# A state-space model rewritten as one real scan, and run as a third stream beside attention and RWKV

## The chip, the cores and the metric

The kernel runs on one core of one Trainium2 chip. The time is that of one execution on the device, in microseconds; the figure used is the median of the runs. Five engines work side by side, each with its own queue in a fixed order: PE (TensorE, matrix products, with its weight loads shown as PEld), DVE (VectorE), ACT (ScalarE), POOL (GpSimd) and SP, which here only starts transfers. A tool that simulates the program's time line puts every instruction into its engine's order when the program is built; on the chip this order doesn't change any more.

## The reference

One layer of a streaming encoder for 1024 prompt tokens and 32 sample tokens (1056 together), in f32. One input projection feeds three mixers; their outputs (384, 256 and 384 columns) go through one output projection, a norm, an MLP with squared ReLU of width 4096, and a second norm.

The mixer that changes is the S5 state-space model: 16 groups of 16 channels, each group with 64 complex states.

```
lam_bar = exp(lam * dt)                       # complex, one per state
x_t = lam_bar * x_{t-1} + B_bar u_t           # per group; zero start for the prompt, state_s5 for the sample
y_t = Re(C x_t) + D u_t
z = gelu(y);  out = z * sigmoid(z @ w_glu + b_glu)
```

The other two are latent attention with 6 heads, chunk-causal over the prompt and over 512 cached keys for the sample, and RWKV-7, a recurrence over a 64 x 64 matrix per head for 6 heads. The last states of S5 and RWKV are outputs too.

## The kernel before

A front part multiplies the input by all weight columns (f32 split in a high and a low half, three products each, `mm3`) and prepares the operands of the three mixers; they are left in DRAM: `u_d` for S5, `rw_d` for RWKV, `q_d` for attention's queries. `stage_s5_params` (L408) works out S5's constants in the same time: the time axis is cut in pieces of `L5` = 8 tokens, so that a group has 128 rows (16 channels x 8 tokens) and `NC5` = 132 columns (128 pieces of the prompt, 4 of the sample). It leaves `em_d` (input piece to state), `cl_d` (state to output piece) and `kt_d` (the kernel inside a piece) in DRAM, and the powers of lam_bar^8 in `g.lp`.

`rwkv_inv` (L764) then inverts the triangular blocks that RWKV needs.

`stage_s5` (L580) follows: all 16 groups at once. It loads `u`, `em`, the blocks `tz0` and `cl`; 16 products (L608) give each piece's contribution to the state, and ACT copies it out of PSUM twice, the second time with the real and imaginary halves of the partitions exchanged (L609, L611). DVE and POOL then run the complex recurrence over 128 pieces as a tree: `fold` (L627) inside runs of 4 and of 16 pieces, eight `advance` steps (L645) across, and back down (L669 to L683). Two products per group (L698, L699) give the output; gelu (L701), a trip through `z_d` that turns the layout, the gate products (L715), sigmoid (L717) and the final product (L719). The pool of this stage lies on the side of memory on which RWKV's pools `rp` and `rl` are opened afterwards.

Then two streams are traced alternately by `side_by_side` (L1291): `a`, `stage_mix`, is attention (233 steps of one tile of scores each: the row maxima of the next head between the outputs of this one); `b`, `stage_streams`, is RWKV (about 124 steps, nine tiles of up to 128 tokens). First `LEAD` steps of `a`, then `RATIO` steps of `a` for one of `b`. The steps of `b` get a higher priority in the planner, and a PE instruction of `a` may be issued only after the last PE instruction that `b` had `SLACK` = 3 steps ago. `attn_past` (L1080) prepares the cached keys. PSUM pools of this part: `psc` (2 buffers: score tiles for the maxima, tag `sc`), `pst` (2: score tiles for the output), `pav` (1) and `pr` (3, RWKV).

Near its end RWKV's stream loads the output weights (`out_weights`) into memory that RWKV no longer uses; `out_early` and `out_mm` start the output projection, and the MLP follows.

What waits on what around the change: RWKV's first loads `ld` (L832) and `xt` (L1030 to L1032) need the memory in which `rwkv_inv` and `stage_s5` worked; attention's memory lies on the other side. SP's queue carries, in one order, S5's loads and stores, RWKV's loads and stores, attention's queries and the row maxima that are written into them (L1246).

## Time and profile before

| | |
|---|---|
| median of 3 runs | 1626.97 us (1623.27 to 1628.03) |
| the profiled execution's own time | 1630.84 us |
| its span, first to last instruction | 1629.1 us |
| PE busy | 1501.1 us, 92% |
| DVE busy | 928.2 us, 57% |
| ACT busy | 501.3 us, 31% |
| POOL busy | 435.8 us, 27% |
| mean granted clock of PE | 0.954 |

The page gives, for each engine, the busy tenths in 40 slices of 40.7 us. The views used below are windows (busy time of each engine in a stretch of the span, with the clock granted to PE and the transfers), groups of instructions (line of the kernel, engine, operation, tiles and shapes; number; busy time and mean; then the idle time before them and what ended it), waits (who waited for whom: us in total, times, longest) and the time line (start, duration, engine, line). A matmul's end is modelled, so a busy PE need not be PE at its peak. An ACT, SP or POOL row with "q" after the name is a transfer being issued.

### The profile page before, as it was taken

The numbers are of one execution on the slowest core, as the hardware profiler recorded it, in microseconds if no ns is written. First come the engines' busy times: TensorE is split into PE (matmuls) and PEld (weight loads), VectorE is DVE, ScalarE is ACT, GpSimd is POOL, SyncE is SP. The second block draws the span as 40 slices with busy tenths as digits, with TensorE's granted clock in tenths as the row PEclk, the third lists the DMA queues.
The fourth block names the chain that finished last, engine by engine and source line by source line (L and its number), as shares of the span: only waits on it lengthen the run. The fifth ranks groups of instructions, "written<-read, shape, count | busy, mean of one in ns | idle before, by whom it ended". The sixth has DMA issues, their size and how long they took to land. (4 is left out here: it accounts for less than half of the span.)

```text
span 1629.1 us, 26187 instructions
## 1 busy us (share of the span) xinstructions
PE 1501.1 (92%) x10855; PEld 1351.0 (83%) x10855; DVE 928.2 (57%) x1644; ACT 501.3 (31%) x953; POOL 435.8 (27%) x385
## 2 busy tenths in 40 slices
PE   7899798957759999899899999999999999999995
PEld 6778797735538777677779999999999999999995
DVE  8535787158824565545765755545544555445457
ACT  4335433251444434343323122221111222221122
POOL 3713751453111021211412112221211122212123
PEclk9989899977789999999999999999999999999998
DMA  5313543540045122213612111111111111111012
GB/s 181 131 56 113 178 119 79 142 126 1 17 115 114 42 76 57 55 38 110 206 46 91 40 39 52 52 42 50 43 48 40 39 53 52 52 40 52 14 40 81
DMA packets 105259, 119.07 MB, mean 73 GB/s; under 512 B 48064, under 2 KB 82548, under 8 KB 104488
## 3 DMA queue, kind: packets, MB, share of 16 engines
q1 hardware_dynamic: 75796, 98.00, 19.8%
q10 hardware_dynamic: 29280, 19.20, 4.0%
q8 instruction: 85, 1.39, 0.3%
q14 instruction: 34, 0.28, 0.1%
q0 software_dynamic: 64, 0.20, 0.0%
HBM read 86.84 MB, written 30.48 MB: 72 GB/s over the span
## 5 line engine op out<-in xcount | busy, mean ns | idle before, releaser
L62 PE MATMUL acc<-xh,uphi 128*128 128x384 f32 (+1 forms) x768 | 248.9, 324 | 0.0
L64 PE MATMUL acc<-xl,uphi 128*128 128x384 f32 (+1 forms) x768 | 247.9, 323 | 0.0
L66 PE MATMUL acc<-xh,uplo 128*128 128x384 f32 (+1 forms) x768 | 247.6, 322 | 0.0
L1510 DVE TENSOR_TENSOR rl<-rl 128x384 f32<-128x384 f32 (+1 forms) x96 | 142.1, 1480 | 176.3 <-ACT rl L1509 174.8
L1538 DVE TENSOR_TENSOR yacc<-yacc,acc 128x384 f32<-128x384 f32 (+2 forms) x344 | 158.7, 507 | 111.8 <-PE acc L66 111.6
L62 PE MATMUL acc<-hh,dnhi 128*128 128x384 f32 (+2 forms) x736 | 209.2, 320 | 0.0
L64 PE MATMUL acc<-hl,dnhi 128*128 128x384 f32 (+2 forms) x736 | 207.1, 319 | 0.0
L66 PE MATMUL acc<-hh,dnlo 128*128 128x384 f32 (+2 forms) x736 | 197.4, 319 | 0.0
L49 POOL TENSOR_TENSOR dnlo<-dnraw,dnhi 128x1024 fp32r<-128x1024 f32 x30 | 72.1, 2404 | 336.4 <-ACT dnhi L48 320.7
L49 POOL TENSOR_TENSOR uplo<-upraw,uphi 128x1024 fp32r<-128x1024 f32 x34 | 82.1, 2416 | 248.7 <-ACT uphi L48 248.7
L62 PE MATMUL acc<-xh,wmhi 128*128 128x384 f32 (+3 forms) x384 | 133.6, 348 | 14.8 <-ACT xh L48 7.9
L62 PEld LDWEIGHTS acc<-xh,uphi 128*128 128x128 f32 x768 | 144.1, 188 | 0.3 <-ACT xh L48 0.3
L64 PEld LDWEIGHTS acc<-xl,uphi 128*128 128x128 f32 x768 | 144.2, 188 | 0.0
L66 PEld LDWEIGHTS acc<-xh,uplo 128*128 128x128 f32 x768 | 144.2, 188 | 0.0
L64 PE MATMUL acc<-xl,wmhi 128*128 128x384 f32 (+3 forms) x384 | 133.4, 348 | 2.7 <-DVE xl L49 2.7
L66 PE MATMUL acc<-xh,wmlo 128*128 128x384 f32 (+3 forms) x384 | 132.3, 345 | 0.0
L64 PEld LDWEIGHTS acc<-hl,dnhi 128*128 128x128 f32 x736 | 131.5, 188 | 0.0
L62 PEld LDWEIGHTS acc<-hh,dnhi 128*128 128x128 f32 x736 | 131.4, 188 | 0.0
L66 PEld LDWEIGHTS acc<-hh,dnlo 128*128 128x128 f32 x736 | 128.9, 188 | 0.0
L48 ACT ACTIVATE dnhi<-dnraw 128x1024 fp32r<-128x1024 f32 x30 | 31.8, 1060 | 298.2 <-PE acc L64 249.2
L48 ACT ACTIVATE hh<-rl 128x384 fp32r<-128x384 f32 (+1 forms) x96 | 47.9, 499 | 148.5 <-DVE rl L1510 148.5
L62 PEld LDWEIGHTS acc<-xh,wmhi 128*128 128x128 f32 (+1 forms) x384 | 74.6, 194 | 20.0 <-ACT xh L48 8.2
(490 smaller groups left out, 2963.7 us busy)
## 6 DMA issues: line engine op xcount, KB each, us to landing
upraw<-in_w_up SPq DMA_DIRECT2D x32, 512.0 KB, 3.6
dnraw<-in_w_dn SPq DMA_DIRECT2D x30, 512.0 KB, 3.6
ld<-rw SPq DMA_DIRECT2D x24, 320.0 KB, 3.9
wmraw<-in_w_m SPq DMA_DIRECT2D x12, 512.0 KB, 3.2
wo<-in_w_out SPq DMA_DIRECT2D x8, 512.0 KB, 3.7
z<-in_xa SPq DMA_DIRECT2D x8, 512.0 KB
out_y<-o SPq DMA_DIRECT2D x8, 512.0 KB, 2.6
xr<-in_xt SPq DMA_DIRECT2D x8, 384.0 KB, 6.3
```

Of the source, the lines that this page charges most:

```text
L48: nc.scalar.activation(out=hi, in_=ps, func=AF.Copy)
L49: (lo_eng or nc.vector).tensor_tensor(out=lo, in0=ps, in1=hi.bitcast(F32), op=ALU.subtract)
L62: nc.tensor.matmul(out=outs[i], lhsT=lh, rhs=rhs[i][0], start=start, stop=False)
L64: nc.tensor.matmul(out=outs[i], lhsT=lh, rhs=rhs[i][1], start=False, stop=False)
L66: nc.tensor.matmul(out=outs[i], lhsT=ll, rhs=rhs[i][0], start=False, stop=stop)
L1510: nc.vector.tensor_tensor(out=r[:, :n], in0=r[:, :n], in1=r[:, :n], op=ALU.mult)
L1538: nc.vector.tensor_tensor(out=y, in0=y, in1=ps[i][:, :n], op=ALU.add)
```

## The change

S5 is written anew as a generator, `stage_s5(g)`, that `stage_mix` steps inside attention's stream: after more than `S5_FROM` = 10 attention steps, one step of it follows every `S5_STEP` = 3rd. It has nine steps in each of its four rounds and ten behind them. It works on `NG` = 4 groups at a time, in four rounds, with one buffer for each of its three large tiles (`ut`: inputs and the blocks inside a piece; `em`: first the input matrix, then the output matrix; `ces`: the table of turns, states and outputs). Its pool lies on attention's side, so RWKV's pools come right behind `rwkv_inv`. `LEAD` goes from 90 to 15, `RATIO` from 1.3 to 2.0.

The recurrence: with lam_bar^8 = rho * e^(i phi), a table holds e^(-i k phi) for every piece k (doubling from 1 to 128, with one Newton step `unit` that keeps the length at 1 before each doubling from the second on). The pieces' contributions are multiplied by it, a real recurrence with rho is run over all pieces and groups by one `tensor_tensor_scan`, and the result is turned back. The columns of a group are the zero start, 128 pieces of the prompt, the sample's start state and 4 pieces of the sample (`NX` = 134; `NY` = 133 of them have an output); a factor of zero in the scan starts the prompt and the sample anew.

S5's PSUM tiles come from attention's `psc`. The output matrix is stored in another order of rows, by which the blocks inside a piece need no re-ordering by ACT; `z_d` is read back in 16 transfers instead of two. Gelu and the two sigmoids each switch ACT's table and back, without making later instructions wait for it (`keep=False`). The old chain of powers at the end of `stage_s5_params` gives way to three squarings of the unit turn. Small tiles move: attention's past tiles into tags `rec` and `rt`, RWKV's `so` into `m`, and the raw halves of every second output weight into S5's tile `ut`.

```diff
@@ -70,12 +70,13 @@
     return g.tc.issue_after(g.le) if g.le is not None else nullcontext()
 
 
-def log_exp_table(g, users):
+def log_exp_table(g, users, keep=True):
 
     pre = g.nc.scalar.preload_act_table_set("natural_log_exp_and_others")
     for u in users:
         g.tc.add_manual_dep(pre.ins, u.ins.name, mybir.DependencyInfo(mybir.DependencyClass.NoSync, mybir.DependencyReason.DATA), reason="table")
-    g.le = pre.ins
+    if keep:
+        g.le = pre.ins
 
 
 def rsqrt_newton(g, m, y, t):
@@ -426,6 +427,7 @@
     dt, mag, ang = t16("dt"), t16("mag"), t16("ang")
     nc.scalar.activation(out=dt, in_=ldt, func=AF.Exp)
     V.tensor_tensor(out=mag, in0=lre, in1=dt, op=ALU.mult)
+    nc.scalar.activation(out=g.rho, in_=mag, func=AF.Exp, scale=float(L5))
     nc.scalar.activation(out=mag, in_=mag, func=AF.Exp)
     V.tensor_tensor(out=ang, in0=lim, in1=dt, op=ALU.mult)
 
@@ -507,8 +509,8 @@
     V.tensor_scalar(out=pis, in0=pi, scalar1=-1.0, scalar2=None, op0=ALU.mult)
     cl = big("cl")
     tb = big("tb")
-    V.tensor_tensor(out=v4t(cl), in0=bc(cst[:, :, None, :], s4), in1=bc(prs[:, :, :, None], s4), op=ALU.mult)
-    nc.gpsimd.tensor_tensor(out=v4t(tb), in0=bc(csw[:, :, None, :], s4), in1=bc(pis[:, :, :, None], s4), op=ALU.mult)
+    V.tensor_tensor(out=v4(cl), in0=bc(cst[:, :, None, :], s4), in1=bc(prs[:, :, :, None], s4), op=ALU.mult)
+    nc.gpsimd.tensor_tensor(out=v4(tb), in0=bc(csw[:, :, None, :], s4), in1=bc(pis[:, :, :, None], s4), op=ALU.mult)
     V.tensor_tensor(out=cl[:, :2048], in0=cl[:, :2048], in1=tb[:, :2048], op=ALU.add)
     nc.scalar.dma_start(out=g.cl_d, in_=cl[:, :2048])
     c0 = sp.tile([P, G5, 16], F32, tag="c0", name="c0", bufs=1)
-    clf = v4t(cl)
+    clf = v4(cl)
@@ -550,174 +552,142 @@
-    pq = big("pq")[:, :512].rearrange("p (a n g) -> p a n g", a=2, n=16)
...
-    for n in (1, 2, 4, 8):
...
-def stage_s5(g, sp):
...
-        return sp.tile([P, G5 * NC5], F32, tag="b5", name=name, bufs=4)
...
-        nc.sync.dma_start(out=tz0[s:P:L5, :, 16 * s:P], in_=g.kt_d[:, :, 0:(8 - s) * 16])
...
-    def fold(x, y, n, c, eng=V):
...
-        V.tensor_tensor(out=t1, in0=x, in1=bcl(lam(n), [P, 2, G5, c]), op=ALU.mult)
...
-            V.tensor_tensor(out=y[:, w], in0=y[:, w], in1=t1[:, w], op=ALU.add)
...
-        fold(e4[:, :, :, :, j - 1], e4[:, :, :, :, j], 1, 32, nc.gpsimd)
...
-        fold(em4[:, :, :, :, 4 * m - 1], em4[:, :, :, :, 4 * m + 3], 4, 8)
...
-        advance(V, "p", ss[:, k + 1], ss[:, k], 16, em4[:, :, :, k, 15])
...
-        advance(nc.gpsimd, "s", sx[:, k + 1], sx[:, k], 1, ee[:, :, :, P + k])
...
-    log_exp_table(g, [nc.scalar.activation(out=zc, in_=zc, func=AF.Gelu_apprx_tanh)])
...
-    log_exp_table(g, [nc.scalar.activation(out=ot, in_=ot, func=AF.Sigmoid) for ot in ots])
...
+    c, q = a2[:, 16:32], a2[:, 0:16]
+    w2 = t16("w2")
+    for n in range(3):
+        V.tensor_tensor(out=w, in0=c, in1=c, op=ALU.mult)
+        V.scalar_tensor_tensor(out=w2, in0=q, scalar=2.0, in1=c, op0=ALU.mult, op1=ALU.mult)
+        V.tensor_tensor(out=q, in0=q, in1=q, op=ALU.mult)
+        V.tensor_tensor(out=c, in0=w, in1=q, op=ALU.subtract)
+        V.tensor_copy(out=q, in_=w2)
+    V.tensor_scalar(out=g.u5[:, 1], in0=q, scalar1=sgn, scalar2=-1.0, op0=ALU.mult, op1=ALU.mult)
+    V.tensor_copy(out=g.u5[:, 0], in_=c)
+    unit(g, g.u5, sp.tile([P, 2, G5], F32, tag="nrm", name="nrm", bufs=1))
+def unit(g, x, t):
+    V = g.nc.vector
+    V.tensor_tensor(out=t, in0=x, in1=x, op=ALU.mult)
+    V.tensor_tensor(out=t[:, 0], in0=t[:, 0], in1=t[:, 1], op=ALU.add)
+    V.tensor_scalar(out=t[:, 0], in0=t[:, 0], scalar1=-0.5, scalar2=1.5, op0=ALU.mult, op1=ALU.add)
+    V.tensor_tensor(out=x, in0=x, in1=bc(t[:, 0:1], list(x.shape)), op=ALU.mult)
+NG = 4
+NX = NC5 + 2
+NY = NC5 + 1
+def stage_s5(g):
+    sp = g.s5
+    for q in range(G5 // NG):
+        gs = slice(NG * q, NG * q + NG)
+        ut = sp.tile([P, NY * L5], F32, tag="ut", name="ut", bufs=1)
+        u = ut[:, :NG * NY].rearrange("p (g k) -> p g k", k=NY)
+        tz = ut[:, NG * NY:NG * NY + NG * P].rearrange("p (g x) -> p g x", x=P)
+        nc.gpsimd.memset(u[:, :, P:P + 1], 0.0)
+        nc.gpsimd.memset(tz, 0.0)
+        src = g.u_d[q // 2][64 * (q % 2):64 * (q % 2) + 64].rearrange("(g c) (t k) -> (c t) g k", c=16, t=L5)
+        nc.sync.dma_start(out=u[:, :, 0:P], in_=src[:, :, 0:P])
+        nc.sync.dma_start(out=u[:, :, P + 1:NY], in_=src[:, :, P:NC5])
+        em = sp.tile([P, NG, P], F32, tag="em", name="em", bufs=1)
+        nc.sync.dma_start(out=em, in_=g.em_d[:, gs])
+        for s in range(8):
+            nc.sync.dma_start(out=tz[s:P:L5, :, 16 * s:P], in_=g.kt_d[:, gs, 0:(8 - s) * 16])
+        ces = sp.tile([P, 4, NG * NX], F32, tag="ces", name="ces", bufs=1)
+        tb = ces.rearrange("p w (g k) -> p w g k", k=NX)
+        e, es = tb[:, 2], tb[:, 3]
+        t1, t2 = (ces[:, 2 + i, :NG * 128].rearrange("p (w g k) -> p w g k", w=2, g=NG) for i in range(2))
+        nc.gpsimd.memset(tb[:, 0, :, 0:1], 1.0)
+        nc.gpsimd.memset(tb[:, 1, :, 0:1], 0.0)
+        V.tensor_copy(out=tb[:, 0:2, :, 1], in_=g.u5[:, :, gs])
+        for n in (1, 2, 4, 8, 16, 32, 64):
+            if n > 1:
+                unit(g, tb[:, 0:2, :, n], sp.tile([P, 2, NG], F32, tag="nrm", name="nrm", bufs=1))
+            x, y = tb[:, 0:2, :, 1:n + 1], tb[:, 0:2, :, n + 1:2 * n + 1]
+            V.tensor_tensor(out=t1[:, :, :, :n], in0=x, in1=bc(tb[:, 0:1, :, n:n + 1], [P, 2, NG, n]), op=ALU.mult)
+            for w in range(2):
+                V.tensor_tensor(out=t2[:, w, :, :n], in0=x[:, 1 - w], in1=bc(tb[:, 1, :, n:n + 1], [P, NG, n]), op=ALU.mult)
+                V.tensor_tensor(out=y[:, w], in0=t1[:, w, :, :n], in1=t2[:, w, :, :n], op=ALU.add if w else ALU.subtract)
+            if n % 3 == 1:
+                yield
+        V.tensor_copy(out=tb[:, 0:2, :, P + 1:NX], in_=tb[:, 0:2, :, 0:5])
+        for j in range(0, NG, 2):
+            ps = g.psc.tile([P, 512], F32, tag="sc", name="s5e")[:, :2 * NY].rearrange("p (j k) -> p j k", k=NY)
+            for i in range(2):
+                nc.tensor.matmul(out=ps[:, i], lhsT=em[:, j + i], rhs=u[:, j + i], start=True, stop=True)
+            nc.scalar.activation(out=e[:, j:j + 2, 1:NX], in_=ps, func=AF.Copy)
+            for i in range(2):
+                nc.scalar.activation(out=es[hsl(1 - i), j:j + 2, 1:NX], in_=ps[hsl(i)], func=AF.Copy)
+            yield
+        nc.gpsimd.memset(tb[:, 2:4, :, 0:1], 0.0)
+        nc.gpsimd.tensor_copy(out=e[:, :, P + 1], in_=g.x0[:, 0, gs])
+        cl = sp.tile([P, NG, P], F32, tag="em", name="cl", bufs=1)
+        nc.sync.dma_start(out=cl, in_=g.cl_d[:, P * NG * q:P * NG * (q + 1)].rearrange("p (g x) -> p g x", x=P))
+        V.tensor_tensor(out=ces[:, 2:4], in0=ces[:, 2:4], in1=ces[:, 0:2], op=ALU.mult)
+        V.tensor_tensor(out=ces[:, 2], in0=ces[:, 2], in1=ces[:, 3], op=ALU.add)
+        nc.scalar.activation(out=es, in_=bc(g.rho[:, gs, None], [P, NG, NX]), func=AF.Copy)
+        nc.gpsimd.memset(es[:, :, 0:P + 2:P + 1], 0.0)
+        V.tensor_tensor_scan(out=ces[:, 2], data0=ces[:, 3], data1=ces[:, 2], initial=0.0, op0=ALU.mult, op1=ALU.add)
+            nc.scalar.activation(out=ces[hsl(1 - i), 3], in_=ces[hsl(i), 2], func=AF.Copy)
+        yield
+        V.tensor_tensor(out=ces[:, 2:4], in0=ces[:, 2:4], in1=ces[:, 0:2], op=ALU.mult)
+        V.tensor_tensor(out=ces[:, 2], in0=ces[:, 2], in1=ces[:, 3], op=ALU.subtract)
+        for i, k in enumerate((P, NX - 1)):
+            nc.gpsimd.tensor_copy(out=g.fin[:, i, gs], in_=e[:, :, k])
+        yo = ces[:, 3, :NG * NY].rearrange("p (g k) -> p g k", k=NY)
+        for j in range(0, NG, 2):
+            ps = g.psc.tile([P, 512], F32, tag="sc", name="s5y")[:, :2 * NY].rearrange("p (j k) -> p j k", k=NY)
+            for i in range(j, j + 2):
+                nc.tensor.matmul(out=ps[:, i - j], lhsT=tz[:, i], rhs=u[:, i], start=True, stop=False)
+                nc.tensor.matmul(out=ps[:, i - j], lhsT=cl[:, i], rhs=e[:, i, 0:NY], start=False, stop=True)
+            nc.scalar.activation(out=yo[:, j:j + 2], in_=ps, func=AF.Copy)
+            yield
+        nc.sync.dma_start(out=g.z_d[gs].rearrange("g x k -> x g k"), in_=yo)
+    so = sp.tile([P, NG, P], F32, tag="em", name="so", bufs=1).rearrange("p a b -> p (a b)")[0:G5, 0:256].rearrange("p (i s r) -> p i s r", i=2, r=2)
+    ps = g.psc.tile([P, 4, P], F32, tag="sc", name="s5l")
+    for i in range(2):
+        nc.tensor.transpose(out=ps[0:16, i], in_=g.fin[:, i], identity=g.ident)
+    yield
+    zt = sp.tile([P, 4, NG * NX], F32, tag="ces", name="zt", bufs=1).rearrange("p a b -> p (a b)")[:, :2 * L5 * NY]
+    zv = zt.rearrange("p (h t k) -> p h t k", h=2, t=L5)
+        for i in range(8):
+            nc.sync.dma_start(out=zv[16 * i:16 * i + 16, h], in_=g.z_d[8 * h + i].rearrange("(t c) k -> c t k", c=16))
+    wg = sp.tile([P, NG, P], F32, tag="em", name="wg", bufs=1).rearrange("p a b -> p (a b)").rearrange("p (k m) -> p k m", k=2)
+    log_exp_table(g, [nc.scalar.activation(out=zt, in_=zt, func=AF.Gelu_apprx_tanh)], False)
+    yield
+    for m in range(2):
+        om = sp.tile([P, NY * L5], F32, tag="ut", name="ot", bufs=1)
+        ot = om.rearrange("p (k t) -> p t k", t=L5)
+            ps = g.psc.tile([P, 512], F32, tag="sc", name="s5g")[:, :n * NY]
+                nc.tensor.matmul(out=ps, lhsT=wg[:, k, m * P:m * P + P], rhs=zt[:, (k * L5 + t) * NY:(k * L5 + t + n) * NY], start=k == 0, stop=k == 1)
+            nc.scalar.activation(out=ot[:, t:t + n], in_=ps.rearrange("p (t k) -> p t k", k=NY), func=AF.Identity, bias=g.vec[:, V_BGLU + m:V_BGLU + m + 1])
+            yield
+        log_exp_table(g, [nc.scalar.activation(out=om, in_=om, func=AF.Sigmoid)], False)
+        V.tensor_tensor(out=ot, in0=ot, in1=zv[:, m], op=ALU.mult)
+        nc.sync.dma_start(out=g.mg_d[3 + m, :, 0:TP], in_=om[:, 0:TP])
+        nc.sync.dma_start(out=g.mg_d[3 + m, :, TP:T], in_=om[:, TP + L5:TP + L5 + TS])
+        yield
@@ -969,7 +939,7 @@
-            so = g.rl.tile([64, 3, P], F32, tag="so", name="so", bufs=1)
+            so = g.rl.tile([P, 3, P], F32, tag="m", name="so", bufs=1)[0:64]
@@ -1074,7 +1044,8 @@
-RATIO, SLACK, PRIO, LEAD = 1.3, 3, 120, 90
+RATIO, SLACK, PRIO, LEAD = 2.0, 3, 120, 15
+S5_FROM, S5_STEP = 10, 3
@@ -1083,13 +1054,13 @@
-    ct = g.ap0.tile([P, 4, P], F32, tag="ct", name="ct")
+    ct = g.ap.tile([P, 4, P], F32, tag="rec", name="ct", bufs=1)
-    kt = g.ap0.tile([P, 4, 32], F32, tag="kt", name="kt")
+    kt = g.ap.tile([P, 4, 32], F32, tag="rt", name="kt", bufs=1)
@@ -1381,7 +1352,7 @@
-        raw = get("wst", 0, 1, dt=F32) if WOUT.index(k) % 2 else get("xt", 0, 3, dt=F32)
+        raw = g.s5.tile([P, NY * L5], F32, tag="ut", name="wo", bufs=1)[:, None, :1024] if WOUT.index(k) % 2 else get("xt", 0, 3, dt=F32)
@@ -1487,7 +1458,14 @@
-        yield from stage_attn(g)
+        ssm, n = stage_s5(g), 0
+        for _ in stage_attn(g):
+            yield
+            n += 1
+            if n > S5_FROM and n % S5_STEP == 0:
+                next(ssm, None)
+        for _ in ssm:
+            yield
@@ -1602,7 +1580,9 @@
-    g.lp = pool.tile([P, 3, 7, G5], F32, tag="lp", name="lp")
+    g.u5 = pool.tile([P, 2, G5], F32, tag="u5", name="u5")
+    g.rho = pool.tile([P, G5], F32, tag="rho", name="rho")
+    g.fin = pool.tile([P, 2, G5], F32, tag="fin", name="fin")
@@ -1623,7 +1603,7 @@
-    g.z_d = dram.tile([16, P, NC5], F32, tag="z_d", name="z_d")
+    g.z_d = dram.tile([16, P, NY], F32, tag="z_d", name="z_d")
@@ -1687,15 +1667,14 @@
+    g.s5 = s0.enter_context(tc.tile_pool(name="s5", bufs=1, reuse_waits="tile"))
-    with tc.tile_pool(name="s5", bufs=1, side="right", reuse_waits="tile") as sp:
-        stage_s5(g, sp)
-    attn_past(g)
+    attn_past(g)
```

122 lines of the change are left out of this document (removed).

## The prediction

> **What bounds the kernel now.** I read the page's slices first, then windows cut at the borders of the stages, then PE's waits. The kernel is bound by TensorE almost everywhere except in the slices from 330 to 490 us.
>
> ```profile
> span 1629.1 us, 26187 instructions
> ...
> PE   7899798957759999899899999999999999999995
> ...
> DVE  8535787158824565545765755545544555445457
> ...
> PEclk9989899977789999999999999999999999999998
> ```
>
> The windows below give, per stage, its length, then the busy time of PE, weight loads (PEld), DVE, ACT and POOL with instruction counts, the granted clock, and DMA. The SSM stage runs from 330 to 482 us beside the first 90 attention steps; RWKV starts at 482; from 490 to 735 RWKV and attention alternate; afterwards RWKV runs out alone.
>
> ```profile
> 330.00:345.00 15.00, 8.19 (x35) 5.22 (x36) 8.43 (x10) 10.08 (x17) 9.99 (x8) 0.77 1.10 327
> 345.00:482.00 137.00, 95.92 (x395) 68.44 (x393) 90.02 (x206) 56.42 (x101) 29.46 (x48) 0.82 0.10 30
> 482.00:490.00 8.00, 2.04 (x14) 1.33 (x14) 0.00 (x0) 0.26 (x1) 4.99 (x5) 0.50 1.28 202
> 490.00:735.00 245.00, 234.03 (x2936) 180.18 (x2931) 138.67 (x328) 104.07 (x234) 43.64 (x78) 0.97 0.25 64
> ```
>
> Until 490 us PE is busy 106.2 of 160 us, at a clock of about 0.82; in the alternating stretch it is busy 234.0 of 245 us (0.955) at 0.97. There the longest wait of PE is small:
>
> ```profile
> PE pry L958 <- ACT yb L937: 7.6, 2, 5.3
> ```
>
> So the early stretch is bound by the SSM's chain over DVE and ACT, the later one by PE. What the change can win is PE's empty time before 490.
>
> **The change, part by part.**
>
> *RWKV from the start, attention's lead cut from 90 steps to 15.* The total PE work is unchanged: same attention and RWKV matmuls; the SSM keeps its 16 state, 32 output and 12 gate products in nearly the same widths (133 columns for 132). The early work is slowed by the clock: 106.2 x 0.82 / 0.97 = 90 us at the later clock. The same score matmul shows it, in the first row before 482, in the second after:
>
> ```profile
> L64 PE MATMUL sc<-kl,qh 128*128 128x512 f32 (+5 forms) x41 | 16.0, 390 | 0.0
> ...
> L64 PE MATMUL sc<-kl,qh 128*128 128x512 f32 (+5 forms) x43 | 14.6, 340 | 0.0
> ```
>
> 90 + 234 = 324 us of work in what are now 405 us (330 to 735). At today's fill of 0.955 that takes 339 us: **-66 us**. At a fill of 1 it is -81; that is the far end.
>
> *The new start.* RWKV's memory now follows the triangular inverse, whose last store is the first row below; today RWKV's first matmul comes 8.1 us after the SSM's last store was issued.
>
> ```profile
> 330.69 3.80 ACTq L813 DMA_DIRECT2D xt_d<-zc  x2
> ...
> 335.19 3.78 PE L1131 MATMUL sck<-ckv,wkv 128*128 128x512 f32 x4 [6.61 <-ACT cpast L1091]
> ...
> 479.83 0.32 SPq L720 DMA_DIRECT2D mg_d<-ot  x1
> ...
> 487.96 0.69 PE L851 MATMUL pra<-ld 64*64 64x128 f32 x4 [13.13 <-DMA ld<-rw]
> ```
>
> 334.5 + 8.1 gives a first RWKV matmul near 343; until then PE has only attention's keys, from 335. Of the 15 us to 345 some 14.3 should be filled and about 4 will be: **+10** (8 to 12).
>
> *The SSM's DVE work.* The old state passes are sixteen DVE groups, 55.0 us in all, 4.1 of them the final gate product, which stays; the largest and the smallest:
>
> ```profile
> L635 DVE TENSOR_TENSOR ee<-ee,t 128x512 f32<-128x512 f32 (+1 forms) x12 | 9.3, 805 | 0.0
> ...
> L672 DVE TENSOR_TENSOR t<-t 128x256 f32<-128x256 f32 x3 | 1.2, 412 | 0.0
> ```
>
> The new work, by size, from these rows:
>
> ```profile
> L565 DVE TENSOR_TENSOR pq<-pq 128x16 f32<-128x16 f32 x1 | 0.2, 168 | 0.0
> ...
> L562 DVE TENSOR_TENSOR pq<-pq 128x64 f32<-128x64 f32 x1 | 0.2, 218 | 0.0
> ...
> L562 DVE TENSOR_TENSOR pq<-pq 128x128 f32<-128x128 f32 x1 | 0.3, 284 | 0.0
> ...
> L491 DVE TENSOR_TENSOR bb<-bb,t 128x256 f32<-128x256 f32 x1 | 0.4, 432 | 0.0
> ...
> L1276 DVE TENSOR_TENSOR rt<-rt,rec 64x512 f32<-64x512 f32 (+1 forms) x13 | 8.0, 617 | 1.6 <-ACT rec L1274 0.9
> ...
> L512 DVE TENSOR_TENSOR cl<-cl,tb 128x2048 f32<-128x2048 f32 x1 | 2.3, 2293 | 0.0
> ...
> L372 DVE TENSOR_TENSOR_SCAN cs<-m,cs x15: 222/675/702, 86.0 to 118.7; 128x260 f32<-128x260 bf16 x12, 128x33 f32<-128x33 bf16 x3
> ```
>
> The table of turns per round of four groups: 24 unit-length ops at 0.17 = 4.0 us; seven doublings with one op of 8 to 512 elements (2.1) and four of half that (6.5); two copies 0.3: 12.9 us. Then two products of 1072 elements (1.2 each), two sums of 536 (0.65), and a scan of 536: 0.22 us for 33 elements and 0.675 for 260 are 2.0 ns an element, so 1.23 us. Together 17.8 a round, 71 for four, 75 with the gate products: 20 us more than now.
>
> When it falls matters more. The SSM takes one step after every third attention step from the twelfth on, 46 steps, so it lives until about step 150 of 233: (150 - 15) / 218 = 0.62 of the shared stretch, some 210 us. DVE has 237.1 - 55.0 = 182 us of other work, 0.62 of it 113; with 75 it is 188 in 210 us, 0.9 of the time. The nearest rows are the five ten-microsecond windows of the present stretch in which DVE is busy over 8.2 us:
>
> ```profile
> 560.00:570.00 10.00, 9.92 (x178) 7.79 (x174) 9.34 (x19) 7.70 (x15) 0.55 (x4) 1.00 0.13 41
> 570.00:580.00 10.00, 8.01 (x80) 5.95 (x82) 8.71 (x22) 3.60 (x11) 4.37 (x5) 1.00 0.54 139
> ...
> 620.00:630.00 10.00, 7.54 (x168) 6.77 (x168) 9.57 (x21) 4.63 (x10) 3.10 (x3) 1.00 0.59 161
> ...
> 650.00:660.00 10.00, 10.00 (x198) 8.72 (x197) 8.24 (x22) 3.39 (x10) 3.43 (x4) 1.00 0.38 100
> ...
> 680.00:690.00 10.00, 7.73 (x156) 6.01 (x154) 8.22 (x12) 4.68 (x8) 5.17 (x6) 1.00 0.28 81
> ```
>
> PE is filled 0.864 in them. The 201 us of PE work (0.62 x 324) take 233 at that fill, 210 at 0.955: 0 to 22 us. As two of the five windows are full, and there will be two attention steps per RWKV step to put between instead of 1.3, I take two thirds: **+15**.
>
> *PSUM shared with attention's scores.* 23 SSM tiles go through the two score buffers, which PE waits for now and then (first row); three ACT copies empty one (the others, for three groups; now two):
>
> ```profile
> PEld sc L62 <- DVE mx L1236: 7.3, 11, 1.5
> ...
> L611 ACT ACTIVATE ee<-fs x12: 272/492/497, 340.9 to 352.0; 64x396 f32<-64x396 f32 x10, 64x132 f32<-64x132 f32 x2
> L609 ACT ACTIVATE ee<-fs x6: 280/500/500, 340.4 to 351.4; 128x396 f32<-128x396 f32 x5, 128x132 f32<-128x132 f32 x1
> ```
>
> 0.3 us more wait for each of 23 at the worst: 0 to 7, I take **+2**.
>
> *ACT tables.* Both gates reload a table and switch back, so six switches for four, now between attention's exponentials:
>
> ```profile
> 452.90 1.96 ACT L701 ACTIVATE zc<-zc 128x2112 f32<-128x2112 f32 x1
> 454.88 1.28 ACT L75 ACT_TABLE_LOAD   x1
> 456.18 1.09 ACT L1265 ACTIVATE ptk<-st 128x512 f32<-128x512 f32 x2
> ```
>
> Two more cost ACT 2.6 us, and ACT is busy about half of the stretch: 0 (to 3). The Trainium skill (ScalarE: Activation LUTs, What ACT_TABLE_LOAD costs) adds a drain of about 1.4 us to every switch, by which six would take some 16 us of ACT and the sum could grow by 8. The trace disagrees: the load begins 0.02 us after the activation before it, and the exponential 0.02 us after the load.
>
> *Queues.* SP gets 13 transfers a round and some 25 at the end, about 75 for 19, eight of a round the strided kernel blocks:
>
> ```profile
> 338.20 8.28 SPq L596 DMA_DIRECT2D tz<-kt_d  x8
> ```
>
> At 1 us each these 32 are 33 us of SP's time. Queued behind one that waits for its buffer are RWKV's tile loads and attention's queries; both are fetched ahead, so 0, and up to +15 without that cover. POOL's clears of the next round's tile wait for the last round's output products, ahead of RWKV's products and attention's masks; DVE's first table operation of a round waits for the last round's output store, which lies in the same tile, ahead of RWKV's masks and sums: both within the same +15, hidden as long as the order on the engines puts these operations late enough. Output weights now pass through the SSM's tile, free since step 150: 0. In the parameter stage the chain of powers gives way to a shorter one; PE is full there, so 0:
>
> ```profile
> 70.00:80.00 10.00, 10.00 (x71) 7.08 (x70) 5.24 (x23) 4.52 (x10) 4.57 (x4) 1.00 0.65 244
> ```
>
> **Sum:** -66 + 10 + 15 + 2 = -39 us. Against the profiled execution's own 1630.8 us (its span and 1.7 around it) that is 1592; it lay 3.9 over the median of 1627.0, so **1588** for the median.
>
> **Rivals.**
> 1. *Even denser.* More independent work per RWKV step fills PE wholly: 324 + 10 = 334 us for 405, -71: 1556. For it: most ten-microsecond rows stand at 10.00 already; against: DVE. Beyond that, PE's busy row may hide room: the weight loads are busy 180.2 of 245 us, and all four windows hold 255 us of them; at 0.955 that is 267 + 10 us, -128: 1499. That is what the Trainium skill says to judge by (Perfetto Trace Analysis, Identifying the Most-Contended Engine: weight-load share, not matmul busy time). Against it, the widest matmul outlasts its weight load by more than two to one:
>
> ```profile
> L1268 PE MATMUL av<-ptk,vo 128*128 128x512 f32 (+5 forms) x142 | 49.7, 450 | 1.6 <-POOL ptk L1267 1.4
> ```
>
> 2. *RWKV does not start early.* Its loads stand on SP behind the SSM's, and attention may not run more than three RWKV steps past its lead: +15, 1603.
> 3. *DVE becomes the bound.* If operations stretch by a quarter when POOL works beside them, 188 becomes 235 us and at 0.9 takes 261 for 210: +51 in place of +15: 1624, no change.
> 4. *Slower: the SSM's chain does not fit its places.* The order on PE is fixed. A round has nine places, 27 attention steps of 339 / 218 = 1.56 us: 42 us. Its chain is 17.8 us of DVE and some 7 of copies and products when alone, but if each of 61 dependent table ops stands behind a foreign one of 0.5 us, about 55. Then PE stands before the state and output products 13 us a round, 52, and 10 before the gates: -39 + 62 = +23: 1650. It decides from 8 us a round. Against: PE loses only 11 us in 245 today with as many crossings.
>
> **Chances.** Forecast (1569 to 1617) 0.63; denser 0.10, hidden room 0.02; late start 0.08; DVE 0.08; slower 0.09. About 0.3% (5 us) is what a measurement can tell from no change. Faster: 0.63 + 0.12 + 0.08 + half of DVE's = 0.87; same 0.04; slower 0.09. The range of 8 in 10 takes the unknown terms (8, 0, 0) to (12, 22, 7, 15) with part of the denser case: 1560 to 1620.
>
> **What would show it.** Right: no stretch of PE below 0.8 between 345 and the merge; RWKV's first matmul near 343; the clock near 0.97; the merge some 39 us earlier; DVE near 0.85 while the SSM lives. Wrong: PE waiting for SSM tiles or evictions for more than 8 us a round, RWKV starting after 360, or DVE operations much over the prices above.

## The result, and the profile after

The changed kernel takes 1640.05 us (median of 19 executions, 1625.45 to 1652.40) against 1626.97 us for the kernel before (19 executions, 1623.27 to 1634.50). The ratio is 1.0066, 95% interval 1.0041 to 1.0091: the change made the kernel slower by about 0.7%. The ratio leaves out the two slowest executions of the changed kernel (1652.40 and 1651.07 us), which count as a slower state; the median of the other 17 is 1637.30 us. The forecast was 1588 us.

The page of the changed kernel, its span, the busy time of TensorE and the slices (the profiled execution took 1648.4 us, its span and 1.8 around it):

```profile
span 1646.6 us, 26449 instructions
PE 1549.7 (94%) x10855; PEld 1372.1 (83%) x10855; DVE 941.1 (57%) x1798; ACT 506.1 (31%) x972; POOL 407.1 (25%) x388
...
PE   7899798868999999998999999999999999999995
...
DVE  8436686477588462444666665455455555455457
...
PEclk9989899879998986798999999999999999999998
```

The hole of the kernel before, the slices from 330 to 490 us, is filled. Yet the same 10855 matmuls, 1501.1 us of busy time before, are now 1549.7 us: TensorE is fuller and gets less done. The windows of the changed kernel show where (columns as in the prediction: length, PE, PEld, DVE, ACT, POOL, granted clock, DMA):

```profile
330.00:345.00 15.00, 3.78 (x4) 1.18 (x4) 14.34 (x39) 5.46 (x8) 6.42 (x6) 0.50 0.86 193
345.00:360.00 15.00, 14.14 (x109) 10.32 (x109) 11.37 (x28) 6.49 (x14) 3.32 (x5) 0.78 0.95 125
360.00:560.00 200.00, 187.96 (x1772) 138.64 (x1772) 136.36 (x421) 85.13 (x190) 22.89 (x75) 0.93 0.25 61
560.00:620.00 60.00, 53.68 (x499) 36.17 (x495) 35.96 (x76) 34.56 (x59) 6.99 (x12) 0.90 0.30 86
620.00:710.00 90.00, 90.00 (x597) 60.32 (x597) 32.86 (x81) 24.55 (x53) 9.46 (x16) 0.77 0.05 15
710.00:780.00 70.00, 62.43 (x576) 44.78 (x576) 34.19 (x64) 29.28 (x60) 12.39 (x21) 0.88 0.30 84
...
490.00:735.00 245.00, 235.35 (x1968) 164.97 (x1968) 126.21 (x322) 100.49 (x203) 32.64 (x66) 0.85 0.19 52
```

The last row answers to the one shown of before: the same 245 us, the same busy time (235.4 for 234.0 us), but 1968 matmuls in place of 2936 and a clock of 0.85 in place of 0.97. The two counts are not of quite the same work: before, all of RWKV came after 488 us, and now part of it lies ahead of the window, so its 64-row matmuls fall from 2231 to 1344. But the rest, attention's for the most part, fall too, from 705 to 624. From 620 to 710 us PE has no idle time at all, the clock is at 0.77, and every other engine is emptier than before (VectorE is busy 32.9 us of it, 52.6 before). So nothing is late there from outside; TensorE itself is slow.

The landmarks, from the rows of RWKV's first tile and of attention's products (engine, line, count, the shortest, median and longest duration in ns, start of the first and of the last):

```profile
L821 PE MATMUL pra<-ld x216: 269/269/473, 347.8 to 707.9; 64*64 64x128 f32 x108
...
L1239 PE MATMUL av<-ptk,vo x204: 190/446/1223, 375.3 to 781.4; 128*128 128x512 f32 x36, 128*128 128x32 f32 x24, 128*128 128x384 f32 x12, 128*128 128x256 f32 x12
```

RWKV begins at 347.8 us (488.0 before). Attention's last product comes at 781.4, where it came at 729.5.

What does TensorE do from 620 us on? Two ten-microsecond windows, then single matmuls from the timeline (start, duration from the first of a group to the end of the last, line, tiles, rows x columns of the array, shape, count):

```profile
620.00:630.00 10.00, 10.00 (x43) 5.17 (x42) 1.76 (x5) 1.75 (x4) 1.84 (x2) 0.50 0.00 0
630.00:640.00 10.00, 10.00 (x32) 5.06 (x32) 1.53 (x4) 0.00 (x0) 0.00 (x0) 0.50 0.00 0
```

```profile
582.71 0.91 PE L928 MATMUL pry<-gq,st 64*64 64x64 f32 x12
583.41 0.60 PE L932 MATMUL prs<-st,gq 64*64 64x64 f32 x12
583.94 0.50 PE L64 MATMUL st<-ql,kh 128*128 128x512 f32 x1
584.27 0.39 PE L66 MATMUL st<-qh,kl 128*128 128x512 f32 x1
584.50 0.34 PE L64 MATMUL st<-ql,kh 128*128 128x384 f32 x1
...
620.90 0.79 PE L62 MATMUL sc<-kh,qh 128*128 128x512 f32 x1
621.50 0.63 PE L64 MATMUL sc<-kl,qh 128*128 128x512 f32 x1
...
622.88 0.79 PE L62 MATMUL st<-qh,kh 128*128 128x512 f32 x1
623.61 0.47 PE L856 MATMUL prn<-r 64*64 64x64 f32 x2
624.01 0.79 PE L64 MATMUL st<-ql,kh 128*128 128x512 f32 x1
624.73 0.47 PE L856 MATMUL prn<-r 64*64 64x64 f32 x2
625.14 0.79 PE L66 MATMUL st<-qh,kl 128*128 128x512 f32 x1
```

In the first five rows RWKV's 64-row matmuls come in blocks: twelve take 0.53 us from start to start (583.41 to 583.94), 0.044 each, and a 512-column matmul of attention 0.23 (584.27 to 584.50). In the last five one attention matmul alternates with two of RWKV's. There a pair of steps takes 1.13 us (622.88 to 624.01). The same three matmuls in blocks would take 0.23 + 2 x 0.044 = 0.32 us, or 0.64 at half clock. So each alternation costs an estimated 0.5 us at half clock, and the clock stays at 0.50 through two windows in which the profile counts PE as busy all the time. Counted in the order of PE's program, RWKV's 64-row matmuls fall into 75 runs in the kernel before and into 180 in the changed one (79 and 184 by the starts in the traces); the order comes from the planner, whose margin PRIO = 120 it is that holds RWKV's groups together.

### The profile page after: what moved, and what is told of

The parts are those of the page before. It is cut to its first block, busy times and chain, and to the rows that moved or that the text cites. A ratio compares the mean times of both kernels' runs of the same rounds, so it can differ in the third digit from the quotient of the medians.

```text
span 1646.6 us, 26449 instructions
## 1 busy us (share of the span) xinstructions
PE 1549.7 (94%) x10855; PEld 1372.1 (83%) x10855; DVE 941.1 (57%) x1798; ACT 506.1 (31%) x972; POOL 407.1 (25%) x388
## 5 line engine op out<-in xcount | busy, mean ns | idle before, releaser
L49 POOL TENSOR_TENSOR dnlo<-dnraw,dnhi 128x1024 fp32r<-128x1024 f32 x30 | 72.4, 2415 | 338.5 <-ACT dnhi L48 323.0
L49 POOL TENSOR_TENSOR uplo<-upraw,uphi 128x1024 fp32r<-128x1024 f32 x34 | 82.3, 2422 | 243.6 <-ACT uphi L48 243.6
```

Source lines behind the costliest of these rows:

```text
L49: (lo_eng or nc.vector).tensor_tensor(out=lo, in0=ps, in1=hi.bitcast(F32), op=ALU.subtract)
```

## The experiments

Theory 1: the margin of 120 instructions no longer holds a group of RWKV's matmuls together, since two attention steps and the SSM's many small operations now lie between two RWKV steps; each cut costs. Theory 2: VectorE's load, or the SSM's chain and its waits, costs more than the forecast's 15 us. Theory 3, the fourth rival of the prediction: the SSM's chain does not fit its places. Each run was compared with executions of the kernel before on the same chip. The differences between runs below are of medians, from several chips; taken by the ratios to the kernel before they shift by up to some 3 us.

**The margin at 400, in the changed kernel**

```diff
-RATIO, SLACK, PRIO, LEAD = 2.0, 3, 120, 15
+RATIO, SLACK, PRIO, LEAD = 2.0, 3, 400, 15
```

> The changed kernel with one number altered: RWKV's priority over attention in the planner is 400 instructions ahead instead of 120. On PE the runs of RWKV's 64x64 matmuls then number 86 instead of 180 (before: 75). Theory 'cuts': what the changed kernel loses is that attention's wide matmuls cut RWKV's runs in pieces, each cut costing PE some 0.25 us at full clock and holding the clock at half for longer: 94 cuts less give 24 us, with the clock 35 to 45, so 1595 to 1616. Rival 'DVE': the SSM's 75 us of DVE work in the shared stretch is what PE waits for; the order on PE does not matter, 1632 to 1645. Rival 'streams': three streams at this ratio leave attention to the end, 1632 to 1645 too.

Measured: 1617.88 us (1614.04 to 1624.82), ratio to before 0.9944 (0.9918 to 0.9970). RWKV's matmuls lie in 86 runs, PE is busy 1494.7 us. The windows of this run:

```profile
330.00:345.00 15.00, 3.64 (x4) 1.18 (x4) 14.41 (x36) 5.68 (x8) 6.89 (x5) 0.61 0.96 196
...
360.00:560.00 200.00, 174.97 (x1922) 137.56 (x1924) 145.85 (x434) 80.50 (x187) 28.13 (x76) 0.91 0.25 62
560.00:620.00 60.00, 44.45 (x390) 28.36 (x385) 24.57 (x48) 31.12 (x49) 7.06 (x13) 0.89 0.27 63
620.00:710.00 90.00, 85.30 (x984) 66.70 (x984) 62.46 (x144) 44.02 (x90) 12.88 (x19) 0.99 0.24 68
```

From 620 to 710 us PE does 984 matmuls in place of 597, more of both kinds (64-row ones 696 for 388, the rest 286 for 208), at 0.99 in place of 0.77. So the cuts cost 22 us by the medians (1640.05 - 1617.88) and 20 by the ratios ((1.0066 - 0.9944) x 1627), a little less than the theory said, and without them the change gains 9. What is left shows too: while the SSM lives, PE is filled 174.97 / 200 = 0.875, and around its gates 44.45 / 60 = 0.74.

**The margin at 0, first in the changed kernel, then in the kernel before**

```diff
-RATIO, SLACK, PRIO, LEAD = 2.0, 3, 120, 15
+RATIO, SLACK, PRIO, LEAD = 2.0, 3, 0, 15
...
-RATIO, SLACK, PRIO, LEAD = 1.3, 3, 120, 90
+RATIO, SLACK, PRIO, LEAD = 1.3, 3, 0, 90
```

> The changed kernel with a priority margin of 0 in place of 120: the same instructions, but RWKV's 64-row matmuls on TensorE fall into 234 runs in place of 180 (86 at a margin of 400, 1617.9 us). If each cut costs what 180 against 86 showed, 0.24 us, the time is near 1653 us. If only one late spell of alternating at half clock made the difference, it stays at 1635 to 1643.

> The kernel before with one number altered: no priority for RWKV (0 instead of 120 instructions). On PE RWKV's 64x64 matmuls then stand in 176 runs instead of 75; nothing of the SSM is changed. Theory 'cuts': about 100 cuts at 0.25 us and some clock lost, 1650 to 1670. Rival 'DVE' or any other cause that lies in the new SSM: within 5 us of before, 1622 to 1632.

Measured: the changed kernel 1651.64 us (1641.87 to 1662.07) with 234 runs of RWKV's matmuls; the kernel before 1678.64 us (1674.43 to 1684.63), ratio 1.0326 (1.0284 to 1.0369), with 176. In the changed kernel the three margins lie near one line: 234 against 180 runs is 11.6 us for 54, 0.21 each; 180 against 86 is 22.2 us for 94, 0.24 each (by the ratios 0.24 and 0.21). That speaks against the one late spell alone, for which 1635 to 1643 was expected; but the four executions at margin 0 scatter by 20 us, and one of them, 1641.87, lies in that range. In the kernel before the same step costs 50 us for 101 runs, 0.5 each, more than was expected; there RWKV also ends 39 us after attention and runs out alone (803.6 against 764.3 us), so the excess over 0.24 is not all cuts.

**Attention's ratio back at 1.3**

```diff
-RATIO, SLACK, PRIO, LEAD = 2.0, 3, 120, 15
+RATIO, SLACK, PRIO, LEAD = 1.3, 3, 120, 15
```

> The changed kernel with 1.3 attention steps per RWKV step, as before, instead of 2.0 (lead still 15). RWKV's runs on PE number 78. Attention then still has some 57 of its 218 steps left when RWKV is through. Theory 'cuts': the runs are whole, so 24 to 45 us less, minus what attention alone at the end costs: 1600 to 1625. Rival 'DVE': the SSM is crowded into the same DVE time per attention step, 1630 to 1650.

Measured: 1619.20 us (1616.12 to 1626.12), ratio 0.9957 (0.9932 to 0.9982), 78 runs. Fewer attention instructions between two RWKV steps bring back the blocks at the margin of 120, and with them nearly the same gain, 21 us by the medians and 18 by the ratios. Two different edits that both bring the number of cuts down to about that of the kernel before give the same time.

**The SSM left out**

```diff
-        ssm, n = stage_s5(g), 0
+        ssm, n = stage_none(g), 0
```

The function put in its place stores zeros where the SSM's outputs go; the margin is 120.

> The changed kernel without its SSM stream: the SSM's scan, its products and its gates are left out, and zeros are stored for its outputs and for its part of the merged rows. RWKV's runs on PE number 100 instead of 180. Theory 'cuts': 80 cuts less (20 us, with the clock 30) and about 35 us of PE work of the SSM gone: 1570 to 1590. Rival 'DVE': 75 us of DVE work gone, so the full gain that was forecast plus the SSM's PE work: 1545 to 1560. If the SSM's presence hardly matters: 1600 or more.

Measured: 1553.58 us (1550.59 to 1558.27), ratio 0.9557 (0.9521 to 0.9594), 100 runs. That lies where the rival 'DVE' put it, below the range of the cuts alone: the cuts are not all that the SSM costs. The SSM costs 64 us over this in the run with the margin at 400, with about as many cuts. Its own matmuls are no more than 30 us, by the groups of the changed kernel:

```profile
L683 PE MATMUL s5g<-zt,wg 128*128 128x399 f32 (+1 forms) x24 | 10.3, 551 | 1.7 <-ACT zt L675 1.7
L653 PE MATMUL s5y<-ut 128*128 128x133 f32 x32 | 7.1, 303 | 0.0
L654 PE MATMUL s5y<-ces,cl 128*128 128x133 f32 x32 | 6.4, 283 | 0.0
L626 PE MATMUL s5e<-ut,em 128*128 128x133 f32 x32 | 5.7, 295 | 0.5 <-ACT ces L629 0.5
```

These rows also hold the waits of PE for the SSM: 1.7 and 0.5 us in all. Theory 3 put them at 13 us a round and 10 before the gates. With the margin at 400 the wait before the gates is longer, as shown below.

**The table of turns left out** (margin 400; the table is filled with ones and zeros)

```diff
-        for n in (1, 2, 4, 8, 16, 32, 64):
-            if n > 1:
-                unit(g, tb[:, 0:2, :, n], sp.tile([P, 2, NG], F32, tag="nrm", name="nrm", bufs=1))
...
+        nc.gpsimd.memset(tb[:, 0, :, 1:P + 1], 1.0)
+        nc.gpsimd.memset(tb[:, 1, :, 1:P + 1], 0.0)
+        for n in range(4):
+            yield
```

> The changed kernel with a priority margin of 400 (1617.9 us before) and the SSM's table of turns left out: it is filled with ones and zeros, so the SSM's outputs are not the reference's; everything else of the SSM, its products, scans, transfers and places, stays. That takes some 52 us of VectorE out of the stretch in which the SSM lives. If VectorE's load in that stretch is what is left of the loss (the stretch from 360 to 560 us has TensorE filled 0.875), the fill goes towards 0.955 and the time to 1590 to 1600. If what is left is the SSM's chain, its gates and the score buffers that it shares, the time stays at 1610 to 1618.

Measured: 1578.02 us (1575.24 to 1580.22), ratio 0.9690 (0.9658 to 0.9722), 80 runs: faster than either expectation. The table costs 40 us (1617.88 - 1578.02), and all the rest of the SSM 24 (1578.02 - 1553.58). As the run without the SSM has 20 cuts more, at 0.21 to 0.24 us each, the rest is some 29 us, about what its matmuls take. The windows of this run beside those of the margin at 400:

```profile
330.00:345.00 15.00, 7.88 (x45) 5.49 (x46) 4.47 (x9) 4.19 (x8) 10.48 (x10) 0.54 1.31 214
...
360.00:560.00 200.00, 187.08 (x2183) 145.90 (x2183) 119.16 (x269) 95.14 (x208) 34.32 (x87) 0.97 0.31 75
560.00:620.00 60.00, 57.55 (x549) 41.21 (x547) 37.89 (x80) 35.18 (x65) 5.08 (x12) 1.00 0.15 47
```

PE gains 4.2 us of busy time at the start, 12.1 from 360 to 560 and 13.1 from 560 to 620, and does 45 + 2183 + 549 matmuls in these windows where it did 4 + 1922 + 390. At the start the reason shows in the DVE column: 36 operations, 14.4 us, stand on VectorE. Some 27 of them (9.6 us) are the first round's table, and attention's keys wait behind most of it: their first operation (`kl`, L49) runs at 339.3 us. Without the table it is 9 operations and 4.5 us.

**Is it VectorE's load or the table's place in the chain?** Four runs. The first keeps only the table and takes the rest of the SSM out; the second leaves the table out and puts as many operations of the same sizes in its place (the one of 512 elements as two of 256), on a tile that nothing else touches; the third moves the table's operations to GpSimd; the fourth gives the transfers at the gates and the stores more time.

The edit of the second run, in the table's loop (margin 400):

```diff
-            V.tensor_tensor(out=t1[:, :, :, :n], in0=x, in1=bc(tb[:, 0:1, :, n:n + 1], [P, 2, NG, n]), op=ALU.mult)
...
+            for k in range(8 * n // m):
+                V.tensor_tensor(out=dm[:, :m], in0=dm[:, :m], in1=bc(dz, [P, m]), op=ALU.mult)
+            for k in range(4):
+                V.tensor_tensor(out=dm[:, :4 * n], in0=dm[:, :4 * n], in1=bc(dz, [P, 4 * n]), op=ALU.mult)
```

That of the third (margin 600), in each operation of the loop:

```diff
-            V.tensor_tensor(out=t1[:, :, :, :n], in0=x, in1=bc(tb[:, 0:1, :, n:n + 1], [P, 2, NG, n]), op=ALU.mult)
+            nc.gpsimd.tensor_tensor(out=t1[:, :, :, :n], in0=x, in1=bc(tb[:, 0:1, :, n:n + 1], [P, 2, NG, n]), op=ALU.mult)
```

And that of the fourth (margin 400):

```diff
         nc.sync.dma_start(out=g.z_d[gs].rearrange("g x k -> x g k"), in_=yo)
+        yield
...
     nc.sync.dma_start(out=wg, in_=g.a["w_glu"])
+    for n in range(4):
+        yield
     log_exp_table(g, [nc.scalar.activation(out=zt, in_=zt, func=AF.Gelu_apprx_tanh)], False)
```

> The changed kernel with a priority margin of 400 in which only the SSM's table of turns is left of the SSM's stream, at the same spacing: its products, scans, transfers and gates are left out, and its outputs are zeros. No product waits for the table. Without any of the SSM the time was 1553.6 us. If VectorE's load by itself is what costs, 1575 to 1585 us; if the SSM costs by its chain, its TensorE work and its waits, 1553 to 1562.

Measured: 1566.27 us (1564.38 to 1570.44), ratio 0.9622 (0.9591 to 0.9653), 89 runs: 12.7 us over no SSM at all, and some 15 if the 11 cuts fewer are counted. Between the two expectations.

> The changed kernel with a priority margin of 400 and the table of turns left out as in the run without the table (1578.0 us; SSM outputs are not the reference's), but with as many VectorE operations of the same sizes a round in its place, in the same steps, on a small tile that nothing else reads or writes, so that they load VectorE and delay no product of the SSM. If VectorE's load costs the 40 us, 1610 to 1620. If the table's place in the SSM's chain costs them, 1578 to 1585. By the two runs so far (the table alone without the rest of the SSM cost 12.7 us, its removal to GpSimd gave back 10.4), about 1590 to 1595.

Measured: 1601.56 us (1600.14 to 1602.59), ratio 0.9839 (0.9820 to 0.9858), 89 runs. Of the 40 us, 23.5 come back with the load alone; 16.3 need the table to be where it is, ahead of the SSM's own products. The 1590 to 1595 that the two runs before it suggested were too low: the table without the rest of the SSM cost only 12.7 to 15, so the load has no fixed price. And with 89 runs of RWKV's matmuls for 80, some 2 of the 23.5 us are cuts. Its windows at the start, while the SSM lives, and around the gates:

```profile
330.00:345.00 15.00, 8.77 (x44) 5.36 (x42) 14.16 (x32) 4.41 (x9) 9.49 (x7) 0.62 1.20 211
...
360.00:560.00 200.00, 178.69 (x1942) 137.49 (x1940) 142.77 (x432) 88.41 (x196) 31.48 (x86) 0.93 0.28 68
560.00:620.00 60.00, 54.53 (x494) 37.80 (x494) 33.42 (x69) 34.35 (x63) 5.11 (x13) 0.94 0.21 62
```

With the same load as the table's (DVE 142.8 us from 360 to 560, 145.9 with the table) PE is filled 0.893 there, against 0.875 with the table and 0.935 without either. But at the start, with the same 14 us on VectorE, PE is busy 8.8 us and not 3.6: the keys' first operation runs at 330.4 us here, ahead of most of the dummy operations. Around the gates PE is busy 54.5 of 60.

> The changed kernel with a priority margin of 600 (RWKV's matmuls in 83 runs, as many as with 400) and every operation of the table of turns moved from VectorE to GpSimd: the same chain of 61 operations a round, each slower there, and 52 us less on VectorE. If VectorE's load is what cost the 40 us, 1580 to 1595. If the length of the chain ahead of the SSM's products is what cost, 1618 or more. In between, both.

Measured: 1607.48 us (1602.03 to 1612.26), ratio 0.9880 (0.9846 to 0.9914), 83 runs. It gives back 10.4 of the 40 us: VectorE is freed, but the chain runs on a slower engine. This agrees with a cost that has both parts, but does not show it: in this run PE also stands 14.4 us for attention's masks on GpSimd (`ptk`), 2.4 in the changed kernel.

> The changed kernel with a priority margin of 400, one step more after each round's output store and four steps more between the loads of the stored outputs and the first gate. With the margin of 400 alone ScalarE stood 10.3 us at the first gate for its loads and VectorE 10.8 us in three places for the output store, with attention's and RWKV's operations queued behind. If these waits at the head of a queue are part of the loss, 1600 to 1610 us; if TensorE finds other work or the waits only move, 1616 to 1620.

Measured: 1617.92 us (1613.08 to 1624.75), ratio 0.9937 (0.9916 to 0.9958), 85 runs: no change against the margin of 400 alone. The two waits that the edit aims at stood in that run's table of ACT's and DVE's waits:

```profile
ACT L675 <- DMA zt<-z_d: 10.3, 1, 10.3
```

```profile
DVE ces L610 <- DMA z_d<-ces: 10.8, 3, 5.5
```

So giving these two more time won nothing in all. The 16 us of the chain are located (the start of the shared stretch and the stretch around the gates), and two of PE's own waits in the run with the margin at 400 name a part of them:

```profile
PE s5g L683 <- ACT zt L675: 9.2, 1, 9.2
PE sck L1102 <- DVE nrm L572: 8.8, 1, 8.8
```

The first is PE before the gates, waiting for gelu's result; it is 3.4 us with the load off the chain. In the run with the gates later it is gone, but PE's waits for attention's exponentials (`ptk`) rose from 2.3 to 10.0 us and those for RWKV's `yb` from 4.6 to 8.6: what the edit gave was taken back elsewhere. The second is attention's first key products, which the profile puts behind an operation of the table. How much of the 16 us each of the two is worth, the runs don't separate.

**The table built once, early** (margin 400, and then margin 200 with ratio 1.3)

The parameter stage builds the table for all sixteen groups by the same doubling, real and imaginary part in two tiles, and stores it; each round of the SSM loads its four groups.

```diff
+    for n in (1, 2, 4, 8, 16, 32, 64):
...
+        V.tensor_tensor(out=R[:, :, hi], in0=R[:, :, lo], in1=c, op=ALU.mult)
+        V.tensor_tensor(out=tv, in0=I[:, :, lo], in1=s, op=ALU.mult)
+        V.tensor_tensor(out=R[:, :, hi], in0=R[:, :, hi], in1=tv, op=ALU.subtract)
...
+    for i, x in enumerate((R, I)):
+        nc.scalar.dma_start(out=g.tb_d[:, i], in_=x)
...
-        for n in (1, 2, 4, 8, 16, 32, 64):
...
+        nc.sync.dma_start(out=tb[:, 0:2], in_=g.tb_d[:, :, gs])
```

> The changed kernel with a priority margin of 400 and the table of turns built once for all sixteen groups in the parameter stage (35 wider groups of VectorE operations, an estimated 26 us by size in place of 52), stored to DRAM and loaded by each round of the SSM. The result is the same. If the table's 52 us on VectorE in the shared stretch are what cost 40 us (1617.9 with them, 1578.0 without), 1578 to 1592 us, the upper end if the parameter stage has no room for 26 us of VectorE there. If leaving the table out won only because nothing had to be waited for at the start of a round, the load of the table takes that place and the time is 1600 or more.

> The kernel with the table built early, with attention's ratio back at 1.3 and a margin of 200 (RWKV's matmuls in 75 runs on TensorE, as in the kernel before the change, in place of 82). If what is left is the number of cuts alone, 1 to 3 us under the kernel with the table built early; if attention left alone at the end (57 us of it at ratio 2.0 and margin 400) cost anything, the same or some us over it, since a lower ratio leaves more of attention for the end.

Measured: 1587.93 us (1586.49 to 1590.62), ratio 0.9766 (0.9741 to 0.9792), 82 runs; with ratio 1.3 it is 1583.11 us (1582.17 to 1583.73), ratio 0.9731 (0.9710 to 0.9752), 75 runs. The first lies within the range of its first reading, 1578 to 1592. The second is the fastest version of the study, 2.7% under the kernel before and 3.5% under the changed one by the medians. The table's operations, fewer and wider, now lie in the parameter stage, where PE stays full (and its clock the same, 0.93 and 0.73, as with the margin at 400 alone); the windows of the first of the two runs:

```profile
80.00:100.00 20.00, 20.00 (x114) 16.13 (x112) 13.42 (x66) 8.70 (x19) 0.23 (x2) 0.93 0.12 35
100.00:120.00 20.00, 20.00 (x77) 15.47 (x76) 10.14 (x19) 5.11 (x10) 4.76 (x7) 0.73 0.14 53
...
360.00:560.00 200.00, 182.64 (x2030) 139.56 (x2030) 114.85 (x253) 100.41 (x213) 26.49 (x72) 0.96 0.31 79
```

The 5 us by which ratio 1.3 is better were put at 1 to 3 by the count of cuts (7 fewer); the cost of attention left for the end, which would have made it slower, did not show.

## Why the prediction was wrong, point by point

**The early hole is worth about what it was put at, as far as the ledger below can tell; the price of the matmuls that fill it was not constant.** The first term, -66 us, took 324 us of PE work at the present clock and the present fill. That supposed that a matmul costs the same in whatever order it stands. This is the step that failed: the edit of ratio and lead in the same change altered the planner's order, RWKV's matmuls fell into 180 runs in place of 75, and the same matmuls cost 48.6 us more of busy time. In wall time the cuts take some 20 us (18 to 22 by the margin at 400 and the ratio at 1.3). The prediction read the number of instructions in the rows and never the order in which the planner would put them, though the diff changes two of its numbers and leaves the third, the margin in instructions, where it was.

The rule that speaks of it was not weighed. The Trainium skill (TensorEngine Tiling (Array Packing), Tiling Modes, Key Properties) says that changing the tiling mode of the array drains it, while going to another tile of the same mode does not. The trace agrees that the change costs: alternating 128-row and 64-row matmuls took an estimated 0.5 us an alternation at half clock, by the rows above, and 0.21 to 0.24 us of wall time per run of matmuls over three margins. That the cost is a drain, no run here shows.

**The new start, +10, held.** RWKV's first matmul came at 347.8 us (343 was said), PE was busy 3.8 of the 15 us to 345 (4 was said) and 14.1 of the next 15. The second rival, a late start, is out.

**VectorE, +15, was mis-sized: its prices were right but for the first round, and its cost was 40.** The rows of the changed kernel for the new operations:

```profile
L636 DVE TENSOR_TENSOR ces<-ces x4: 1257/1274/1276, 371.3 to 525.3; 128x1072 f32<-128x1072 f32 x4
L637 DVE TENSOR_TENSOR ces<-ces x4: 690/700/708, 373.0 to 526.8; 128x536 f32<-128x536 f32 x4
L640 DVE TENSOR_TENSOR_SCAN ces<-ces x4: 1274/1275/1853, 374.7 to 529.0; 128x536 f32<-128x536 f32 x4
...
L571 DVE TENSOR_TENSOR nrm<-ces x24: 148/172/449, 313.3 to 517.4; 128x8 f32<-128x8 f32 x24
```

1.27, 0.70, 1.28 and 0.17 us were put at 1.2, 0.65, 1.23 and 0.17. But the 61 table operations of the first round, from 309 to 349 us, took 27.4 us, where the other three rounds took 12.9 to 14.5. GpSimd prepares attention's operands at that time, and an operation of VectorE that falls beside one of GpSimd can last as long as that one:

```profile
310.47 2.42 DVE L615 TENSOR_TENSOR ces<-ces 128x8 f32<-128x8 f32 x1
310.45 2.40 POOL L1172 TENSOR_TENSOR qropeb<-qropeb,ropec 64x1056 f32<-64x1056 f32 x1
```

The same eight elements take 0.17 us in the last two rounds. Over all 244 table operations of the changed kernel, the 47 with GpSimd busy for more than half of their time took 2.7 times the median of their kind, the 189 with it busy for less than a tenth 0.98 times.

The fill of 0.864 that the five busy windows gave was right too: 0.875 with the margin at 400. What failed is the step after it, "I take two thirds", and what it left out. The load alone costs 23.5 us, a little over the upper bound of 22; the place of the table in the SSM's chain another 16.3: at the start of the stretch, where the first table holds VectorE before attention's keys, and around the gates. The third rival, VectorE as the bound, comes near the size of the cost (+51 was said in place of +15, and 40 was measured) and has its reason in part: beside GpSimd the operations do stretch, 69 us for the table in place of 53 at the medians, but nearly all of it in the first round, and from 360 to 560 us VectorE was 0.68 to 0.73 busy and not 0.9. What the stretch is worth of the 40 us, no run separates.

**The score buffers (+2), the ACT tables (0) and the queues (0)** together cannot be large: without the table, all of the SSM costs 24.4 us over no SSM, some 29 with the difference in cuts, and its matmuls alone are 29.5 us in the groups above.

**The fourth rival had the sign and the size and not the mechanism.** 1650 was its time, 1640 the measured one, and that is luck: PE's waits for the SSM's tiles are 2.2 us in the changed kernel. The largest waits of PE in the shared stretch are others, and small:

```profile
PE sck L1102 <- DVE kl L49: 6.7, 1, 6.7
PE prs L932 <- ACT yb L907: 5.3, 2, 3.8
PE pry L928 <- ACT yb L907: 4.1, 2, 2.5
```

A wrong expectation of waits would have been seen here; an order that makes PE slow leaves no wait at all. Only when the cuts are gone (margin 400) does the wait before the gates come up, 9.2 us of the 10 that the rival gave it; the 13 us a round do not (0.5 us in all). Of the signs named for "right", RWKV's start held within 5 us, and PE stayed over 0.8 in the windows above, though single ten-microsecond ones fall to 0.63. The clock "near 0.97" failed (0.85), and so did VectorE near 0.85 (0.68) and the merge 39 us earlier: the first product with the output weights came at 756.2 us, 737.6 before.

**The ledger.** 1640.05 less the cuts (22.2) is 1617.9; less the table (39.9: 23.5 of load, 16.3 of place) is 1578.0. The forecast without its DVE term was 1573. So these two terms make 47 of the 52 us of the miss (1640 - 1588): 22 of cuts, 20 by the ratios, of which the prediction knew nothing, and 40 - 15 = 25 of the table. The other 5 stay open, and so does the -66 by itself, which no run measures alone.

## What to carry to other kernels

When a change alters how two streams are mixed, read the order of the instructions that the planner gives, not only their number: a margin in instructions that keeps groups whole loses its meaning as soon as the streams' steps get longer. A busy engine is not a fast one: divide the count of matmuls of one kind by the window, and look at the granted clock, before calling PE the bound. Serial small operations are best built once, in a stage whose bound is another engine; here 244 of them in the shared stretch cost 40 us, and built for all groups at once in the parameter stage, in fewer and wider operations, they gave back 30.

## What the runs showed of the hardware

- TensorE stayed at half clock while the profile counted it busy for the whole of two ten-microsecond windows (43 and 32 matmuls in 10 us). The Trainium skill (TensorE: Matmul & The Clock Gate, Part 1: The HAM clock gate) has the clock released after some 3.4 us of sustained busy time; here 20 us of what the profile calls busy did not release it, so the time in which the array is held between two modes seems not to count as activity. At 640.3 us the alternation gives way to nine matmuls of attention in a row, and the clock of the window from 640 to 650 us is 0.75, so it came back within that window. The reading is argued from these rows, not tested by itself.
- How much of the 0.21 to 0.24 us a cut is the change between the two kinds itself and how much the clock that falls with it, the runs don't separate.
- The executions of the changed kernel scatter more than those of the kernel before (27 us against 11), and its mean granted clock with them: the execution of 1626.0 us had 0.956, that of 1649.4 us had 0.942.
- Small operations of VectorE took 2.7 times as long with GpSimd busy beside them (47 table operations of the changed kernel), and 0.98 times without it (189).
- With some 52 us (by their prices) of dependent small operations, VectorE at 0.7 of its time already costs PE: 0.893 of fill with a load that nobody waits for, 0.935 without it.
